# A hybrid encoder layer on one core: one value block in three split, the last key products beside the first score blocks, and pauses ahead of the gate products

## The chip, the cores and the metric

The kernel runs on one core of one Trainium2 chip. The metric is device time in microseconds (us) of one execution, lower is better. The kernel before takes 1352.38 us, the median of three runs (1351.4 to 1353.75).

The core has five engines that work through their own queues in order: TensorE (PE; its weight loads are shown as PEld), VectorE (DVE), ScalarE (ACT), GpSimd (POOL) and SyncE (SP, which only issues transfers here). Sixteen DMA engines move data. TensorE writes to PSUM, the other engines read it from there.

## The reference

One encoder layer is applied to two sequences of 256 tokens of width 1024, with 16 learned tokens put ahead of each. All data are float32.

```python
def layer(h, ...):
    xn = rmsnorm(h, norm_mix_g)
    z = xn @ w_in                                    # convolution gates and inputs, q, k, v
    y_conv = group_rmsnorm(gate_b * depthwise_conv3(gate_c * hc, conv_w), conv_out_g, 8)
    y_attn = group_rmsnorm(gqa_attention(q, k, v), attn_out_g, 8)   # normed, rotated q and k
    h = h + concatenate([y_conv, y_attn]) @ w_out
    return h + peer_ffn(rmsnorm(h, norm_ffn_g), ...)

def peer_ffn(x, wq, subkeys, u_tab, v_tab):          # 8 heads, 128 x 128 experts
    q = (x @ wq).reshape(T, 8, 2, 128)
    s = einsum('thpc,hpnc->thpn', q, subkeys)        # 128 scores for each half of a head
    sv, si = top_k(s, 16)
    cand = sv[..., 0, :, None] + sv[..., 1, None, :]
    cv, cp = top_k(cand, 16)                         # 16 experts of 16384, for each head
    gates = softmax(cv)
    a = gelu(einsum('thkd,td->thk', take(u_tab, eidx), x)) * gates
    return einsum('thk,thkd->td', a, take(v_tab, eidx))
```

The tables u_tab and v_tab hold 16384 rows of 1024 numbers each, 64 MB a table. Each token needs 128 of the experts (8 heads of 16).

## The kernel before

**Two ways to the experts.** The first sequence (two tiles of 128 tokens) gathers: for each tile and each of the 128 picks, one indirect transfer on GpSimd's queue (line 180, tile `grow`) brings for every token the row of u and v of its expert, 128 rows of 8 KB. VectorE then forms the dot product with the token (`grow<-grow,xh`), ScalarE its gelu and the weight (two small instructions on `dots`), and VectorE adds the weighted v row (`xh<-grow,dots,xh`). There are 256 such gathers, and they run in the background of all later stages. Four buffers hold rows in flight (`ring`). A new gather is issued once a buffer is free and TensorE has passed a mark (`sync_dep`, the last matmul that the program had recorded).

The second sequence goes through all experts, with dense matmuls. In the score stage (the loop over `j` that starts at line 975), block j multiplies the 128 experts of row j with the 256 tokens: eight matmuls of 128 x 256, each shown as two records, into one of two PSUM tiles `pSj` that hold four blocks (`SG`). After each fourth block ScalarE takes the gelu of four blocks at once into the big table A (its parts are `Al`, the first 92 blocks, and `Ah`). In the value stage (the loop at line 1023) block j multiplies A(j) with 128 rows of v into four PSUM accumulators `acc`. SyncE brings the weights: `u` in blocks of 512 KB, `v` in pairs of blocks of 1 MB, in three buffers.

**The gates** make the dense way sparse: for each token A is to be multiplied with a matrix that is zero but for its 128 experts. The generator `gates_dense` (line 883) builds it from one-hot matrices. First, `fin1` softmaxes and decodes the picks of both tiles. Then, for each tile of 128 tokens, the index tables are transposed on TensorE (`pi`, `pg`) and copied to `dup`, `ghi` and `glo`. Then come 32 steps of four tokens: VectorE compares (`oi`, `oj`), ScalarE scales (`gh`, `gl`), and a step later TensorE multiplies eight small matrices into `pgm`. After each second step the result is either stored into A (ScalarE, blocks that have no scores yet) or multiplied into A (VectorE, blocks that have).

**What sets the order.** The program issues instructions in the order that it writes them, and a scheduler changes it a little. Background work is paced by credit: `bg(us)`, called after each block with 3.5, gives `us * share["b"]` to the task list (generators, each `yield` names the time that its piece takes) and `us * share["a"]` to the gathers, one per 2.65 of credit. A task's piece therefore lands a number of blocks later that its yields set: with `SBS` = 0.42 a block gives 1.47, so that a yield of 3.0 is worth about two blocks.

**The queries of the second sequence** come ahead of the scores, in `projections` (line 376). For each of 16 half heads, eight matmuls make a query (`pqq`), and two, three half heads later (`lag=3`), the key scores (`pn`, line 385), which ScalarE copies to `Ah`, and after every second of which `step1` puts the top-16 search of a head on VectorE. The three late ones are done after the loop, by `while late`.

**Split value blocks.** Most value blocks use four float32 matmuls of 128 x 512, each shown as two records. Each `SPL`-th block is split instead: ScalarE rounds A(j) and v to the float32r format (`ah`, `vh`, the tile `vhl`), VectorE makes the rests (`al`, `vl`), and TensorE multiplies three terms, twelve float32r matmuls. The splitting of block j is issued one block ahead, ahead of that block's gathers.

Of the kernel before, what the change touches and what calls it, by code (L numbers as in the profile page):

```python
# [8 lines left out]
F32 = mybir.dt.float32  # L9
# [9 lines left out]
P = 128  # L19
# [20 lines left out]
SR = 0.6  # L40
SS = 0.72
SMAX = 0.74
SPL = 4
SBS = 0.42


# [1 line left out]
def encoder_layer(ctx: ExitStack, tc: tile.TileContext, xp, xs_, meta, vec, w_in, w_out, wq,  # L48
# [328 lines left out]
    def projections(xr, sk, scores, qp, step=None, split=False, rescale=None, lag=1):  # L377

        rn = None
        late = []  # L380

        def key_scores(hp, qs):
            pn = pst.tile([P, 2, P], F32, tag="tr", name="pn")
            for t in range(2):
                pe.matmul(pn[:, t, :], qs[:, t * P:(t + 1) * P], sk[:, hp, :], start=True, stop=True)
            if hp < 2 and rn is not None:
                for t in range(2):
                    act.activation(scores[:, hp, t], pn[:, t], AF.Copy, scale=rn[:, t:t + 1])
            else:
                act.activation(scores[:, hp], pn, AF.Copy)  # L390
            if step is not None and hp % 2:
                step(hp // 2)

        for hd in range(PH):
            w = weights(wq, hd, split)
            for pp in range(2):
                pq = psm.tile([P, 256], F32, tag="mm", name="pqq")
                mm(pq, lambda c, k: w(c, k)[:, pp * P:(pp + 1) * P], xr, split=split)
                qs = qp.tile([P, 256], F32, tag="qs", name="qs", bufs=lag + 1)
                act.activation(qs, pq, AF.Copy)  # L400
                late.append((2 * hd + pp, qs))
                if len(late) > lag:
                    key_scores(*late.pop(0))
                if hd == 0 and rescale is not None:
                    rn = rescale(xr, pp)
                bg(3.9)
        while late:
            key_scores(*late.pop(0))


    pf = ExitStack()
# [459 lines left out]
        return rn1  # L871

    share.update(a=SR, b=0.0)
    projections(xr1, sk1, sc1, q1, step1, rescale=rescale, lag=3)
    direct[0] = True
    pfs.close()
    psS = ctx.enter_context(ps("psS", 2))
# [5 lines left out]
    def gates_dense():  # L883

        for t in range(2):
            yield from fin1(t)
        q1x.close()
        topk_left[0] = -1
        yield 10.0
        ogx = ExitStack()  # L890
        og = ogx.enter_context(sb("og", 1, "right"))
        io = og.tile([P, P], F16, name="io")
        act.dma_start(io, iota16)
        ident16 = og.tile([P, P], F16, name="ident16")
        act.activation(ident16, ident, AF.Copy)
        iv = io.rearrange("p (a r) -> p a r", r=2)
        v4 = lambda x: x.rearrange("p t (a r) -> p t a r", r=2)
        steps = []
        pgs = [None]

        def gate_products(a, oi, gh, gl):
            half = a // OC % 2
            if half == 0:
                pgs[0] = psg.tile([P, 2 * OC, P], F32, tag="g", name="pgm")
            pg = pgs[0]
            for r in range(OC):
                q = half * OC + r
                pe.matmul(pg[:, q, :], oi[:, r, :], gh[:, r, :], start=True, stop=False)  # L908
                pe.matmul(pg[:, q, :], oi[:, r, :], gl[:, r, :], start=False, stop=True)  # L909
            if half == 0:  # L910
                return
            a -= OC
            n = r_done[0]
            pj = pg.rearrange("p t j -> p j t")
            parts = [(part, lo, hi, min(max(n, lo), hi)) for part, lo, hi in ((Al, 0, JH), (Ah, JH, P))]
            for part, lo, hi, m in parts:
                if m < hi:
                    act.activation(part[:, m - lo:hi - lo, a:a + 2 * OC], pj[:, m:hi], AF.Copy, scale=1.0 / GSH)
            for part, lo, hi, m in parts:
                if m > lo:  # L920
                    av = part[:, 0:m - lo, a:a + 2 * OC]
                    dve.scalar_tensor_tensor(av, pj[:, lo:m], 1.0 / GSH, av, op0=ALU.mult, op1=ALU.mult)
            tau[0] = a + 2 * OC

        for t in range(2):
            pi = psg.tile([P, 2, P], F16, tag="g", name="pi")
            pe.transpose(pi[:, 0, :], idx_i[:, t], ident16)
            pe.transpose(pi[:, 1, :], idx_j[:, t], ident16)
            pg = psg.tile([P, P], F32, tag="g", name="pg")
            pe.transpose(pg, gate_all[:, 2 + t], ident)  # L930
            glo = og.tile([P, P], F32, tag="glo", name="glo")
            g16 = og.tile([P, OC, P], F16, tag="gl", name="g16", bufs=2)[:, 0, :]
            dup = og.tile([P, 2, P, 2], F16, tag="dup", name="dup")
            ghi = og.tile([P, P], F32, tag="ghi", name="ghi")
            act.activation(g16, pg, AF.Copy, scale=GSH)
            dve.scalar_tensor_tensor(glo, pg, GSH, g16, op0=ALU.mult, op1=ALU.subtract)
            act.activation(ghi, g16, AF.Copy)
            for r in range(2):
                act.activation(dup[:, 0:2, :, r], pi, AF.Copy)
            yield 1.6  # L940
            for o in range(P // OC):
                s0 = o * OC
                oi = og.tile([P, OC, P], F16, tag="oi", name="oi", bufs=2)
                oj = og.tile([P, OC, P], F16, tag="oj", name="oj", bufs=2)
                gh = og.tile([P, OC, P], F16, tag="gh", name="gh", bufs=2)
                gl = og.tile([P, OC, P], F16, tag="gl", name="gl", bufs=2)
                sl4 = lambda k: dup[:, k, s0:s0 + OC, None, :].to_broadcast([P, OC, 64, 2])
                ib = iv[:, None, :, :].to_broadcast([P, OC, 64, 2])
                dve.tensor_tensor(v4(oi), sl4(0), ib, op=ALU.is_equal)
                dve.tensor_tensor(v4(oj), sl4(1), ib, op=ALU.is_equal)  # L950
                for q in range(OC):
                    act.activation(gh[:, q, :], oj[:, q, :], AF.Copy, scale=ghi[:, s0 + q:s0 + q + 1])
                    act.activation(gl[:, q, :], oj[:, q, :], AF.Copy, scale=glo[:, s0 + q:s0 + q + 1])
                steps.append((t * P + s0, oi, gh, gl))
                if len(steps) > 1:
                    gate_products(*steps.pop(0))
                yield 1.3 + (4 * r_done[0] + 60) / 700
        gate_products(*steps.pop(0))
        ogx.close()

    tasks.append(gates_dense())
    share.update(a=SS, b=SBS)
    late = []

    def experts(j, p):
# [12 lines left out]
    for j in range(P):  # L978
# [7 lines left out]
        mm(late[-1][1][:, j % SG], lambda c, k: ub[:, c * P:(c + 1) * P], xr1)  # L986
        if j % SG == 0 and j:
            experts(*late.pop(0))
        bg(3.5)
    experts(*late.pop(0))  # L990
    run_tasks()
# [121 lines left out]
```

## Time and profile before

| | |
|---|---|
| median of three runs | 1352.38 us |
| the profiled execution | 1352.28 us, span 1350.5 us |
| TensorE | busy 1275.4 us (94%), 5998 records |
| VectorE | busy 1043.2 us (77%) |
| ScalarE | busy 536.2 us (40%) |
| GpSimd | busy 387.4 us (29%) |
| granted TensorE clock, mean | 0.984 |
| moved by DMA | 460.19 MB, 341 GB/s over the span |
| chain that ended last | TensorE 51%, DMA 10%, VectorE 8% of the span |

The times count from the start of the span. The first sequence's layer ends with its queries; the second sequence's layer follows, its queries end at 408, the scores run to 924, the values to 1345. Shares over the whole span say little here, since the stages have different limits; stretches and single waits are to be read. In a timeline row the number ahead of the engine is the duration (of several records together where the row ends with a count), and what stands in brackets is the idle time of the engine just before it and what ended it. The record of a matmul is longer than the time between two starts, since matmuls overlap.

### The profile page before, as it was taken

To read this page: it belongs to the slowest core of one execution; us is meant where nothing else is said; L and a number is where in the kernel's file an instruction comes from. 1 tells how busy PE (TensorE), PEld (TensorE's weight loads), DVE (VectorE), ACT (ScalarE), POOL (GpSimd) and SP (SyncE) were. 2 spreads that over 40 slices of the span, in tenths; PEclk is the share of its full clock that TensorE was granted. 3 is DMA by queue.
4 is the path that set the end of the run, shared out by engine and by line. 5 is a ranking of instruction groups with operands and counts; after the bars stand their busy time and mean duration, and the time that the engine had idled before them with its cause. 6 is when DMAs were issued, how large, how long until landed. Compare 5 with 4: busy or idle time off the path is not lost.

```text
span 1350.5 us, 17724 instructions
## 1 busy us (share of the span) xinstructions
PE 1275.4 (94%) x5998; PEld 957.6 (71%) x5998; DVE 1043.2 (77%) x2247; ACT 536.2 (40%) x1576; POOL 387.4 (29%) x480
## 2 busy tenths in 40 slices
PE   5999998888898999779999999998999999999998
PEld 5888996667787887668788888885555555555554
DVE  5656998976699998688887978986767667676665
ACT  4555531752221311176776766641222222222121
POOL 1111124432242334434332322332222223223121
PEclk9999998998998999979999999999999999999999
DMA  5434646576998999999999999999999999999997
GB/s 204 131 103 159 205 123 228 203 267 255 374 326 293 365 418 416 417 383 413 386 405 387 416 408 400 404 413 421 404 403 396 406 401 405 404 395 408 400 402 283
DMA packets 81003, 460.19 MB, mean 341 GB/s; under 512 B 9473, under 2 KB 9985, under 8 KB 39697
## 3 DMA queue, kind: packets, MB, share of 16 engines
q0 software_dynamic: 37296, 270.02, 49.9%
q1 hardware_dynamic: 41888, 183.37, 36.1%
q10 hardware_dynamic: 1728, 5.67, 1.2%
q8 instruction: 47, 0.77, 0.2%
q14 instruction: 44, 0.35, 0.1%
HBM read 454.81 MB, written 4.19 MB: 340 GB/s over the span
## 4 chain that ended last, share of the span: by engine, by line
PE 51%; DMA 10%; DVE 8%; issue 1%; ACT 1%; POOL 0%; DVEq 0%; POOLq 0%
PE acc L1029 30%; PE pSj L138 19%; DMA grow<-in_uv,eidx 10%; DVE Al L65 2%; DVE xh L65 2%; DVE grow L65 2%; PE pgm L908 1%; PE pgm L909 1%; DVE Ah L65 1%; DVE s L65 0%; POOL cd L294 0%; ACT dots L65 0%; DVE c L65 0%; DVE hd L65 0%; ACT gh L65 0%
## 5 line engine op out<-in xcount | busy, mean ns | idle before, releaser
L180 POOL DMA_INDIRECT grow<-in_uv,eidx x256 | 310.6, 1213 | 733.2 <-PE acc L1029 229.7
L138 PE MATMUL pSj<-xr,u 128*128 128x256 f32 x2048 | 468.7, 386 | 4.6 <-ACT Al L65 2.7
L138 PEld LDWEIGHTS pSj<-xr,u 128*128 128x128 f32 x2048 | 387.5, 193 | 62.8 <-DMA u<-in_u_t 6.4
L65 DVE SCALAR_TENSOR_TENSOR grow<-grow,xh 128x1024 f32<-128x1024 f32 x256 | 312.7, 1221 | 143.3 <-DMA grow<-in_uv,eidx 141.9
L65 DVE SCALAR_TENSOR_TENSOR xh<-grow,dots,xh 128x1024 f32<-128x1024 f32 x256 | 328.1, 1282 | 62.9 <-ACT dots L65 61.8
L65 ACT ACTIVATE dots<-dots 128x1 f32<-128x1 f32 x256 | 51.8, 202 | 525.2 <-DVE grow L65 524.3
L1029 PE MATMUL acc<-v,Al 128*128 128x512 f32 x552 | 240.7, 593 | 0.7 <-DMA v<-in_v_n 0.7
L1029 PEld LDWEIGHTS acc<-v,Al 128*128 128x128 f32 x552 | 104.9, 190 | 123.8 <-issue 120.8
L65 ACT ACTIVATE gh<-oj,ghi 128x128 f16<-128x128 f16 x256 | 99.7, 389 | 8.3 <-PE pgm L908 4.7
L65 ACT ACTIVATE gl<-oj,glo 128x128 f16<-128x128 f16 x256 | 99.7, 389 | 0.0
L1029 PE MATMUL acc<-v,Ah 128*128 128x512 f32 x216 | 94.2, 592 | 0.0
L1029 PE MATMUL acc<-vhl,ah 128*128 128x512 f32 x256 | 81.7, 441 | 2.8 <-ACT vhl L65 2.8
L65 ACT ACTIVATE dots<-dots,gate_all 128x1 f32<-128x1 f32 x256 | 74.7, 292 | 6.8
L1029 PEld LDWEIGHTS acc<-v,Ah 128*128 128x128 f32 x216 | 41.1, 190 | 48.0 <-issue 47.3
L1029 PEld LDWEIGHTS acc<-vhl,ah 128*128 128x128 f32 x256 | 48.1, 188 | 26.1 <-issue 14.8
L65 DVE TENSOR_TENSOR wlo<-w,whi 128x1024 fp32r<-128x1024 f32 x42 | 50.9, 1216 | 18.6 <-PE pc L138 11.3
L138 PE MATMUL pqq<-xr,w 128*128 128x256 f32 x256 | 58.1, 380 | 2.9 <-DMA w<-in_wq 1.8
L65 ACT ACTIVATE vhl<-v 128x1024 fp32r<-128x1024 f32 x32 | 33.8, 1056 | 53.9 <-DMA v<-in_v_n 51.4
L138 PEld LDWEIGHTS pqq<-xr,w 128*128 128x128 f32 x256 | 47.6, 190 | 9.3 <-DMA w<-in_wq 2.2
L65 ACT ACTIVATE whi<-w 128x1024 fp32r<-128x1024 f32 x42 | 43.8, 1054 | 17.0 <-PE pqq L138 9.5
L138 PE MATMUL pc<-xT,w 128*128 128x258 f32 (+1 forms) x192 | 47.4, 398 | 2.9 <-DVE rb L65 2.4
L908 PE MATMUL pgm<-gh,oi 128*128 128x128 f16 x256 | 36.3, 221 | 14.1 <-ACT gh L65 11.4
(278 smaller groups left out, 1724.5 us busy)
## 6 DMA issues: line engine op xcount, KB each, us to landing
u<-in_u_t SPq DMA_DIRECT2D x128, 512.0 KB, 8.5
v<-in_v_n SPq DMA_DIRECT2D x64, 1024.0 KB, 9.1
w<-in_w_in SPq DMA_DIRECT2D x36, 512.0 KB, 4.6
w<-in_wq SPq DMA_DIRECT2D x32, 512.0 KB, 4.7
w<-in_w_out SPq DMA_DIRECT2D x16, 512.0 KB, 4.0
grow<-in_uv,eidx POOLq DMA_INDIRECT x256, 9.7
hdram<-h ACTq DMA_DIRECT2D x3, 512.0 KB, 4.1
h<-in_xp SPq DMA_DIRECT2D x2, 512.0 KB
```

The costliest lines, as they stand in the source:

```text
L65: i = f(*a, **k)
L138: i = pe.matmul(out, st_(c, a), mv(c, b), start=(n == 0), stop=(n == NC * len(terms) - 1))
L180: i = pool.indirect_dma_start(out=r, out_offset=None, in_=uv, in_offset=bass.IndirectOffsetOnAxis(ap=eidx[:, t, k:k + 1], axis=0))
L908: pe.matmul(pg[:, q, :], oi[:, r, :], gh[:, r, :], start=True, stop=False)
L909: pe.matmul(pg[:, q, :], oi[:, r, :], gl[:, r, :], start=False, stop=True)
L1029: i = pe.matmul(acc[t][q], a[:, t * P:(t + 1) * P], v[:, q * 512:(q + 1) * 512], start=j == 0 and n == 0, stop=j == P - 1 and n == len(ter ...
```

## The change

Three edits. (1) `SPL` becomes 3: value blocks 2, 5, 8, ..., 125 are split, 42 in place of 32. (2) `projections` with a lag over 1 returns its late key scores as a function; the score loop calls it after blocks 0, 1 and 2, into the PSUM pool of the gates. The gates task and its shares are set after block 3. (3) The yield ahead of the gates' tables falls from 10 to 6, and two yields are added for each tile of tokens, 3.0 ahead of its first step and 2.0 behind its first step.

```diff
-SPL = 4
+SPL = 3
...
-        def key_scores(hp, qs):
-            pn = pst.tile([P, 2, P], F32, tag="tr", name="pn")
+        def key_scores(hp, qs, pl=None, tag="tr"):
+            pn = (pl or pst).tile([P, 2, P], F32, tag=tag, name="pn")
...
-        while late:
-            key_scores(*late.pop(0))
+        if lag > 1:
+            return lambda pl, tag: late and key_scores(*late.pop(0), pl, tag)
+        key_scores(*late.pop(0))
...
-    projections(xr1, sk1, sc1, q1, step1, rescale=rescale, lag=3)
+    rest = projections(xr1, sk1, sc1, q1, step1, rescale=rescale, lag=3)
...
         topk_left[0] = -1
-        yield 10.0
+        yield 6.0
...
             yield 1.6
+            yield 3.0
             for o in range(P // OC):
...
                     gate_products(*steps.pop(0))
+                if o == 0:
+                    yield 2.0
                 yield 1.3 + (4 * r_done[0] + 60) / 700
...
-    tasks.append(gates_dense())
-    share.update(a=SS, b=SBS)
     late = []
...
             experts(*late.pop(0))
+        if j < 3:
+            rest(psg, "g")
+        if j == 3:
+            tasks.append(gates_dense())
+            share.update(a=SS, b=SBS)
         bg(3.5)
```

What this does to the order is read from the two programs. First TensorE, from the first score block to the second set of gate products of the first tile (`pSj` x8 is one score block, `pi` and `pg` are the transposes, `pgm` the gate products). Before:

```order
L138 MATMUL pSj<-xr,u 128x256 x312
L927 LDWEIGHTS idx_i
L927 MATMUL pi<-ident_5105,idx_i 128x128
L928 LDWEIGHTS idx_j
L928 MATMUL pi<-ident_5105,idx_j 128x128
L930 MATMUL pg<-ident,gate_all 128x128
L138 MATMUL pSj<-xr,u 128x256 x16
L908 LDWEIGHTS oi
L908 MATMUL pgm<-gh,oi 128x128
```

After, with the last key scores (`pn`) among the first blocks:

```order
L138 MATMUL pSj<-xr,u 128x256 x16
L385 MATMUL pn<-Ah,qs 128x128
L138 MATMUL pSj<-xr,u 128x256 x8
L385 MATMUL pn<-Ah,qs 128x128 x2
L138 MATMUL pSj<-xr,u 128x256 x296
L928 LDWEIGHTS idx_i
L928 MATMUL pi<-ident_5103,idx_i 128x128
L929 LDWEIGHTS idx_j
L929 MATMUL pi<-ident_5103,idx_j 128x128
L931 MATMUL pg<-ident,gate_all 128x128
L138 MATMUL pSj<-xr,u 128x256 x40
L909 LDWEIGHTS oi
```

One more score block stands ahead of the transposes (40, not 39) and five stand between them and the first gate products, where two stood. The key scores, of which two instructions make a half head, come behind blocks 1 and 2 in part.

On ScalarE the same place is the one where the transposes' results are copied (`dup`, `ghi`); `Al<-pSj` is the gelu of blocks 36 to 39, each pair of `dots` belongs to one gather, `gh` and `gl` are the scalings of the first step. Before:

```order
L65 ACTIVATE dots<-dots 128x1
L65 ACTIVATE dots<-dots,gate_all 128x1
L65 ACTIVATE dup<-pi 128x256
L65 ACTIVATE g_5113<-pg 128x128
L65 ACTIVATE dup<-pi 128x256
L65 ACTIVATE ghi<-g_5113 128x128
L65 ACTIVATE dots<-dots 128x1
L65 ACTIVATE dots<-dots,gate_all 128x1
L65 ACTIVATE Al<-pSj 128x1024
L65 ACTIVATE dots<-dots 128x1
L65 ACTIVATE dots<-dots,gate_all 128x1
L65 ACTIVATE gh<-oj,ghi 128x128
```

After:

```order
L65 ACTIVATE dots<-dots 128x1
L65 ACTIVATE dots<-dots,gate_all 128x1
L65 ACTIVATE Al<-pSj 128x1024
L65 ACTIVATE g_5111<-pg 128x128
L65 ACTIVATE dup<-pi 128x256
L65 ACTIVATE ghi<-g_5111 128x128
L65 ACTIVATE dup<-pi 128x256
L65 ACTIVATE dots<-dots 128x1
L65 ACTIVATE dots<-dots,gate_all 128x1
L65 ACTIVATE dots<-dots 128x1
L65 ACTIVATE dots<-dots,gate_all 128x1
L65 ACTIVATE gh<-oj,ghi 128x128
```

The copies of the transposes stood ahead of that gelu and now stand behind it; counted from the gelu of blocks 32 to 35, four gathers' pairs stood ahead of it and now five do; and two pairs stand between the copies and the first scaling, as before.

The third place is VectorE at the change from scores to values. `Al<-pgm` and `Ah<-pgm` multiply gate products into A, `Ah<-pSj` multiplies the gelu of new blocks with the gates that are there, `al` and `vhl` are the rests of the first split value block. Before, from the last gate products on:

```order
L65 SCALAR_TENSOR_TENSOR Al<-pgm,Al 128x92x8
L65 SCALAR_TENSOR_TENSOR Ah<-pgm,Ah 128x28x8
L65 SCALAR_TENSOR_TENSOR xh<-grow,dots,xh 128x1024
L65 SCALAR_TENSOR_TENSOR grow,dots<-grow,xh 128x1024
L65 TENSOR_TENSOR al<-Al,ah 128x256
L65 SCALAR_TENSOR_TENSOR xh<-grow,dots,xh 128x1024
L65 SCALAR_TENSOR_TENSOR grow,dots<-grow,xh 128x1024
```

After:

```order
L65 SCALAR_TENSOR_TENSOR grow,dots<-grow,xh 128x1024
L65 SCALAR_TENSOR_TENSOR xh<-grow,dots,xh 128x1024
L65 SCALAR_TENSOR_TENSOR grow,dots<-grow,xh 128x1024
L65 SCALAR_TENSOR_TENSOR Al<-pgm,Al 128x92x8
L65 SCALAR_TENSOR_TENSOR xh<-grow,dots,xh 128x1024
L65 SCALAR_TENSOR_TENSOR grow,dots<-grow,xh 128x1024
L65 TENSOR_TENSOR Ah<-pSj,Ah 128x4x248
L65 SCALAR_TENSOR_TENSOR Ah<-pgm,Ah 128x36x8
L65 TENSOR_TENSOR al<-Al,ah 128x256
L65 TENSOR_TENSOR vhl<-v,vhl 128x1024
L65 SCALAR_TENSOR_TENSOR xh<-grow,dots,xh 128x1024
```

Before, nine gathers' pairs and the gelu products of eight blocks came between the last gate products and the first `vhl`; now one pair does, and the last gate products stand at the very end of the score stage.

## Rows read from the trace of the kernel before

**Rows 1.** Stretches: length, PE, PEld, DVE, ACT, POOL busy (records), clock, DMA share, GB/s.

```profile
480.00:560.00 80.00, 78.87 (x348) 63.98 (x347) 66.55 (x96) 14.81 (x49) 35.07 (x22) 1.00 1.02 416
560.00:585.00 25.00, 10.63 (x37) 7.54 (x36) 20.06 (x28) 9.57 (x33) 10.58 (x8) 0.73 1.01 410
920.00:960.00 40.00, 36.57 (x105) 19.38 (x104) 27.87 (x34) 9.44 (x26) 9.14 (x9) 1.00 1.01 419
960.00:1320.00 360.00, 360.00 (x997) 188.69 (x996) 244.65 (x305) 77.80 (x219) 94.47 (x83) 1.00 1.00 402
480.00:1320.00 840.00, 818.34 (x3361) 569.11 (x3360) 646.18 (x904) 333.56 (x1095) 256.00 (x209) 0.99 1.00 404
```

**Rows 2.** Timeline of TensorE, last key scores: start, us, operation, count, idle time ahead.

```profile
412.18 2.93 PE L385 MATMUL pn<-Ah,qs 128*128 128x128 f32 x12 [3.46 <-ACT Ah L65]
415.58 4.76 PE L138 MATMUL pSj<-xr,u 128*128 128x256 f32 x16 [0.47 <-ACT Ah L65]
```

**Rows 3.** Timeline of TensorE around the first gate products.

```profile
564.46 5.41 PE L138 MATMUL pSj<-xr,u 128*128 128x256 f32 x16 [2.73 <-ACT Al L65]
...
581.31 0.27 PE L908 MATMUL pgm<-gh,oi 128*128 128x128 f16 x1 [11.44 <-ACT gh L65]
...
583.42 9.59 PE L138 MATMUL pSj<-xr,u 128*128 128x256 f32 x32
...
593.29 3.67 PE L138 MATMUL pSj<-xr,u 128*128 128x256 f32 x16
```

**Rows 4.** Timeline of ScalarE in the same place.

```profile
559.54 0.20 ACT L65 ACTIVATE dots<-dots 128x1 f32<-128x1 f32 x1 [3.21 <-DVE grow L65]
...
563.29 0.20 ACT L65 ACTIVATE dots<-dots 128x1 f32<-128x1 f32 x1 [3.23 <-DVE grow L65]
563.40 1.01 ACT L65 ACTIVATE Al<-pSj 128x1024 f32<-128x1024 f32 x1
...
580.87 0.39 ACT L65 ACTIVATE gh<-oj,ghi 128x128 f16<-128x128 f16 x1
```

**Rows 5.** Timeline of TensorE at the second hole.

```profile
640.32 3.67 PE L138 MATMUL pSj<-xr,u 128*128 128x256 f32 x16
646.33 0.24 PE L908 MATMUL pgm<-gh,oi 128*128 128x128 f16 x1 [2.34 <-DVE oi L65]
...
647.11 5.02 PE L138 MATMUL pSj<-xr,u 128*128 128x256 f32 x16
```

**Rows 6.** Timeline of TensorE, change from scores to values.

```profile
899.12 24.39 PE L138 MATMUL pSj<-xr,u 128*128 128x256 f32 x112
924.16 10.57 PE L1029 MATMUL acc<-v,Al 128*128 128x512 f32 x24 [0.65 <-DMA v<-in_v_n]
937.51 1.21 PE L1029 MATMUL acc<-vhl,ah 128*128 128x512 f32 x4 [2.77 <-ACT vhl L65]
```

**Rows 7.** Timeline of VectorE, the last gate products multiplied into A.

```profile
900.30 0.91 DVE L65 SCALAR_TENSOR_TENSOR Al<-pgm,Al 128x736 f32<-128x736 f32 x1
```

**Rows 8.** Timeline of TensorE, one period of four value blocks.

```profile
953.46 10.46 PE L1029 MATMUL acc<-v,Al 128*128 128x512 f32 x24
963.36 1.48 PE L1029 MATMUL acc<-vhl,ah 128*128 128x512 f32 x4
964.68 1.08 PE L1029 MATMUL acc<-vhl,al 128*128 128x512 f32 x4
...
966.51 1.02 PE L1029 MATMUL acc<-v,Al 128*128 128x512 f32 x2
```

**Rows 9.** Timeline of ScalarE and VectorE, the splitting for that period.

```profile
956.20 1.06 ACT L65 ACTIVATE vhl<-v 128x1024 fp32r<-128x1024 f32 x1 [0.74 <-DMA v<-in_v_n]
...
959.16 1.22 DVE L65 TENSOR_TENSOR vhl<-v,vhl 128x1024 fp32r<-128x1024 f32 x1
960.29 0.42 DVE L65 TENSOR_TENSOR al<-Al,ah 128x256 fp32r<-128x256 f32 x1
```

**Rows 10.** Transfers issued: engine, count, size, median us from issue to landing.

```profile
v<-in_v_n SPq DMA_DIRECT2D x64, 1024.0 KB, 9.1
```

## What I predicted

> **What bounds the kernel now.** I read the table of stretches first [rows 1]. From 480 to 1320 us TensorE is busy for 818.34 of 840 us and the DMA engines are full too, at 404 GB/s. Two limits lie on top of each other, and the question for any edit is which of them has room. From 960 to 1320 TensorE is busy all the time: the value stage is bound by its matmuls. From 560 to 585 it is busy for 10.63 of 25 us, and there is the only large hole.
>
> Next I read TensorE in order of time around that hole [rows 3]. Score block 40 starts 2.73 us late, for ScalarE; the first gate product waits 11.44 us more; and the two score blocks from 583.42 take 9.59 us, where one block is recorded at 3.67 [rows 5]. The granted clock of 560 to 585 is 0.73, so part of this stretch runs at the lower of the two levels, behind idle time. The place costs 2.73 + 11.44 + (9.59 - 7.34) = 16.4 us. A smaller hole follows [rows 5]: 2.34 us of waiting and a block of 5.02 us in place of 3.67, 3.7 us in all.
>
> Then ScalarE in the same place [rows 4]. It works in order. Between its large evictions (the gelu of four score blocks, 1.01 us) stands a small pair of instructions for each gather, which waits for VectorE, which waits for the gather's transfer. These pairs come 3.75 us apart (559.54, 563.29), which with the score weights beside them is about the 416 GB/s of 480 to 560 [rows 1], the highest rate that holds for long. So ScalarE runs late, TensorE has only two buffers of four score blocks, and it stands until ScalarE comes. The hole is TensorE's, and DMA makes it.
>
> Last I read the change of stages [rows 6, 7] and one period of the value stage [rows 8, 9].
>
> **The change part by part.** The sum is made against the profiled execution, 1352.28 us (span 1350.5 and 1.78 around it). The median of the runs shown is 1352.38, so one number serves for both.
>
> *Key products.* Before, the last of them hold TensorE from 412.18 to 415.58 [rows 2], 3.4 us, since each pair waits for ScalarE to empty one of two PSUM tiles. Now five instructions of key scores stand ahead of the first block, not eight, and three come between the first blocks (order on TensorE); the first block should start near 413.5. I cost the 1 to 2 us won at nothing: at block 40 TensorE waits for ScalarE anyway [rows 3], whose date comes from the gathers, and in ScalarE's order 68 gathers stand ahead of the gelu of blocks 32 to 35 in both kernels. Bounds: 2 us won (the wait at block 40 gone), 1 lost (top-k work on VectorE that gets its scores three blocks later).
>
> *Start of the gates.* The transposes come after 40 blocks, not 39, and the first gate products after 45, not 41. The gelu of blocks 32 to 35 ends at 564.4 as before, so block 40 starts there in both. Blocks 40 to 43 then fill TensorE until about 579, in the place of the long wait. Block 44 needs the gelu of blocks 36 to 39, which now has five gather pairs ahead of it, not four: 563.29 + 5 x 3.75 = 582.0, so block 44 starts near 583.3 after a wait of 4 us, and ends at 587. The first gate products need the scalings gh, which stand two gathers later, 582.0 + 7.5 = 589.5, and from the first scaling to the end of the set it takes 583.42 - 580.87 = 2.5 us: 592.0, with 45 blocks done. Before, block 45 began at 593.29 + 2 x 3.92 = 601.1 (3.92 from the 12 blocks between 593.29 and 640.32 [rows 3, 5]), with three more sets of gate products done, 3.92 - 3.48 = 0.44 each (3.48 from seven blocks without them in 24.39 us [rows 6]). So 601.1 - 592.0 - 1.3 = 7.8 us are won of 16.4.
>
> What is late next is the same chain. The second hole stands behind 92 gathers before; at the same block 89 stand ahead now (order on ScalarE), since a longer task lets gathers slip. Three gathers of 3.75 us are 11.2 us of relief, so what is won can be kept, but the 3.7 us are hardly closed as well. To the end of the scores 3 to 4 gathers fewer stand ahead of each gelu. I take 8 us. Bounds: 0 (ScalarE decides as before) and 16.4 + 3.7 = 20.1 (both holes gone).
>
> *Queues that are passed.* Gathers on GpSimd are held by marks of TensorE, and score weights on SyncE by buffers that TensorE frees; both follow it and come earlier by what it wins. Behind ScalarE's wait for the transposes' result stand gather pairs; they wait there before as well.
>
> *End of the scores.* The gates' last step, which stood seven blocks ahead of the values, now stands directly ahead of them (order on VectorE). Before, the change of stages cost 0.65 us for DMA and 2.77 us for ScalarE, 3.4 us [rows 6]. Now the first value block needs the last gate product and VectorE's multiply of 0.91 us [rows 7], behind up to two gathers in VectorE's order; the first split block is one block nearer to the start, but while TensorE waits for the multiply its copy can be made. I put both at 3.4 us, the difference at 0, since the 3.4 is the nearest row. Bounds: 3.4 won, and 8 lost (a wait as the 11.44 us at the first gate products).
>
> *Value blocks.* 42 blocks are split, not 32. In the split block the last eight matmuls take 966.51 - 964.68 = 1.83 us, 0.23 each, so twelve take 2.75. The period of four blocks is 966.51 - 953.46 = 13.05 us, so an unsplit block takes (13.05 - 2.75) / 3 = 3.43 us [rows 8]. Ten blocks at 0.68 are 6.8 us. Read by starts alone (963.36 - 953.46 = 9.90 for three, 3.15 for one) it would be 10 x 0.15 = 1.5 us. I take the first reading, since a start at a change of kind seems recorded early.
>
> The Trainium skill (FP8 and Floating Point Precision, section TensorE Precision Notes) says that true FP32 takes four passes through the array. By it three terms would take 3/4 of 3.43 us, and ten blocks would save 8.6 us; the 2.75 us measured are more than that 2.57, and the measurement is taken.
>
> What the splits cost: each adds 1.06 us on ScalarE and 1.22 + 0.42 on VectorE [rows 9], 11 and 16 us in a stage where these are busy 77.80 and 244.65 of 360 us: covered. But blocks 2, 8, 14, ... are the first of a pair that one transfer brings; before, the split one was always the second. In [rows 9] the pair landed at 956.20, VectorE had the last part at 960.71, 4.5 us later, and TensorE came to it at 963.36. The pair's first block was due 3.43 us sooner, at 959.93, and its second term 0.9 later, at 960.85. So at 21 places the margin falls to some 0.1 us, and I count 0.1 us lost at each. DMA: a block needs 0.524 MB of values and 97/126 of a gather of 1.049 MB in 9.61/3 = 3.20 us, 416 GB/s, where 94/126 in 3.26 us made 401 (402 measured). 416 and 419 are the highest rates of [rows 1], so it just fits. I take 4 us won; bounds 6.8 won, 5 lost (0.55 us at each of 21 places).
>
> **Sum:** 0 + 8 + 0 + 4 = 12 us; 1352.3 - 12 = 1340 us.
>
> **Rivals.** *DMA takes it all back.* For it: full engines at 404 GB/s. Against: 416 holds for 80 us. If 404 is the most that this mixture gives, each wait returns elsewhere, and the time is 1352. If 416 is, the room is 840 x (1 - 404/416) = 24 us, above the sum. Chance 0.11.
>
> The Trainium skill (HBM Reference, section Specifications (TRN2)) gives about 425 GB/s to a core that streams alone. By it the room would be 42 us; no row here shows more than 419.
>
> *The pauses do too little.* ScalarE is no earlier against TensorE, because its gathers decide; only the values gain: 1352.3 - 4 = 1348. Against: four blocks of work do lie in the hole now. Chance 0.12.
>
> *All holes close.* 20.1 + 6.8 + 1, cut to the room of 24 us: 1328. Against: 73 gathers cannot be served by 579. Chance 0.14.
>
> *Slower: split blocks that come first in their pair starve.* It decides as soon as a pair lands about 1 us later against its use than in [rows 9]: 10 us after its issue where the median is 9.1 [rows 10]. At 1.2 us at each of 21 places 25 us are lost against 8 + 6.8 won: 1363. Against: a TensorE that waits frees DMA, so that the next pair lands sooner. Chance 0.07.
>
> **How the numbers follow.** The forecast has 0.56. The range, 1328 to 1352, reaches from all holes closed to nothing won; perhaps 0.07 lie below and 0.11 above. The likeliest case alone spans 1334 to 1346. A difference under 0.2%, 2.7 us, cannot be told from none. Faster: 0.56 + 0.14 + 0.10 of the second rival = 0.80. Same: 0.10 of the first and 0.02 of the second, 0.12. Slower: 0.07 and 0.01 of the first, 0.08.
>
> **What would show it.** In the changed profile the wait of 11.44 us at the first gate products should be gone, with one of 3 to 5 us at block 44 and one of 3 to 5 us at the first gate product in its place. The first score block starts near 413.5, and block 40 still near 564. The value stage lasts some 416 us where it lasted 420, at DMA rates of 410 to 419. Wrong would be: a wait of over 8 us at the start of the values; many short waits of TensorE for vhl or al; or block 40 itself earlier or later by more than 3 us.

## The result and the profile after

The changed kernel takes 1347.88 us, the median of 20 runs, where the kernel before took 1355.24 us beside it (20 runs). The ratio is 0.995, with a 95% interval of 0.9934 to 0.9966: by the ratio 6.8 us won, 4.6 to 8.9 by the interval (the two medians lie 7.4 apart). I had forecast 12. The direction was right and the measured time lies inside the range, but the size was wrong. The profiled execution took 1349.14 us, its span is 1347.4, 3.1 us below the one before.

The table of stretches of the changed kernel answers to [rows 1]; one stretch is added (900 to 920).

```profile
480.00:560.00 80.00, 78.83 (x349) 64.92 (x348) 66.72 (x96) 15.19 (x48) 32.89 (x21) 1.00 1.02 416
560.00:585.00 25.00, 19.82 (x83) 16.56 (x82) 17.79 (x22) 6.31 (x20) 12.09 (x8) 0.86 1.02 417
900.00:920.00 20.00, 19.74 (x121) 17.25 (x119) 18.09 (x27) 13.16 (x46) 5.86 (x6) 1.00 0.91 340
920.00:960.00 40.00, 32.76 (x87) 17.67 (x88) 27.76 (x36) 8.76 (x27) 9.63 (x8) 0.87 0.92 368
960.00:1320.00 360.00, 359.57 (x1041) 196.40 (x1041) 263.07 (x331) 89.71 (x244) 96.09 (x86) 1.00 1.01 413
480.00:1320.00 840.00, 818.94 (x3409) 579.27 (x3408) 659.41 (x926) 344.89 (x1112) 257.57 (x209) 0.99 1.00 405
```

Between 560 and 585 TensorE is busy for 19.82 us, before for 10.63: most of the hole is filled. Between 900 and 920 DMA moves 340 GB/s, where the kernel before moved 417. Between 920 and 960 TensorE is busy for 32.76, before for 36.57, and DMA has fallen from 419 to 368 GB/s: a new hole, and not one that full DMA engines make.

TensorE around the first gate products, where [rows 3] showed the wait of 11.44 us (bracket: idle time ahead and what ended it):

```profile
566.30 16.37 PE L138 MATMUL pSj<-xr,u 128*128 128x256 f32 x64 [4.34 <-ACT Al L65]
583.52 3.72 PE L138 MATMUL pSj<-xr,u 128*128 128x256 f32 x16 [0.84 <-ACT Al L65]
590.43 0.22 PE L909 MATMUL pgm<-gh,oi 128*128 128x128 f16 x1 [3.19 <-ACT gh L65]
592.53 4.83 PE L138 MATMUL pSj<-xr,u 128*128 128x256 f32 x16
...
642.18 7.13 PE L138 MATMUL pSj<-xr,u 128*128 128x256 f32 x32
```

Blocks 40 to 43 now run through what was the wait, slowly: 16.37 us for four, with a granted clock of 0.86 from 560 to 585. Waits of 4.34 us (block 40, before 2.73), 0.84 (block 44, which starts at 583.52) and 3.19 (the first gate product, at 590.43) are left. The last row stands where the second hole was [rows 5]; there is none, two blocks take 7.13 us.

ScalarE in the same place, against [rows 4]: the gelu of blocks 36 to 39 and the first scaling.

```profile
582.46 1.00 ACT L65 ACTIVATE Al<-pSj 128x1024 f32<-128x1024 f32 x1
...
589.99 0.39 ACT L65 ACTIVATE gh<-oj,ghi 128x128 f16<-128x128 f16 x1
```

The change from scores to values, against [rows 6]: TensorE, from the last gate product to the first split block.

```profile
919.52 0.22 PE L910 MATMUL pgm<-gl,oi 128*128 128x128 f16 x1
927.24 9.86 PE L1036 MATMUL acc<-v,Al 128*128 128x512 f32 x16 [7.50 <-DMA v<-in_v_n]
936.54 1.50 PE L1036 MATMUL acc<-vhl,ah 128*128 128x512 f32 x4
...
949.34 7.03 PE L1036 MATMUL acc<-v,Al 128*128 128x512 f32 x16
955.80 1.48 PE L1036 MATMUL acc<-vhl,ah 128*128 128x512 f32 x4
957.12 1.08 PE L1036 MATMUL acc<-vhl,al 128*128 128x512 f32 x4
958.04 1.08 PE L1036 MATMUL acc<-vhl,ah 128*128 128x512 f32 x4
958.96 7.03 PE L1036 MATMUL acc<-v,Al 128*128 128x512 f32 x16
```

Where 0.65 us of waiting for `v` stood, 7.50 us stand now. The first two value blocks also take 9.30 us (927.24 to 936.54), and two later ones 6.46 (949.34 to 955.80), 2.8 more. From 949.34 on, one period of three blocks takes 958.96 - 949.34 = 9.62 us.

Why `v` came late is read from SyncE. Its first issue of `v` in the timeline of the kernel before:

```profile
910.16 13.71 SPq L1009 DMA_DIRECT2D v<-in_v_n  x3
```

In the changed kernel, its longest wait between 900 and 930 us (total, times, longest), and the issue in the timeline:

```profile
SPq L1016 <- PE pgm L910: 15.4, 1, 15.4
```

```profile
919.81 1.46 SPq L1016 DMA_DIRECT2D v<-in_v_n  x3
```

Before, the first pair was issued at 910.16, right behind the last score weights and 13.4 us ahead of the scores' end at 923.51. Now it waits 15.4 us for the last gate product and leaves at 919.81, when the scores are over. The addresses in the program say why. The gates' pool lies at 148416 to 159168 bytes of each partition, and the first of the three `v` buffers at 150976 to 159168, in that same memory. Before, the gates were done seven blocks earlier, so the lock (as I call the wait of a new tile for the last use of its memory) was open by the time SyncE came to it.

VectorE in the same place, against [rows 7]:

```profile
921.53 0.92 DVE L65 SCALAR_TENSOR_TENSOR Al<-pgm,Al 128x736 f32<-128x736 f32 x1
...
924.70 1.18 DVE L65 TENSOR_TENSOR Ah<-pSj,Ah 128x992 f32<-128x992 f32 x1
925.80 0.45 DVE L65 SCALAR_TENSOR_TENSOR Ah<-pgm,Ah 128x288 f32<-128x288 f32 x1
```

The accumulators `acc` lie in the PSUM that the `pgm` tiles leave, so the first value product also has to wait until VectorE has read the last of these. The last multiply out of it ends at 926.25, only 1.0 us ahead of TensorE's start. A second lock stands right behind the first.

### The profile page after: what moved, and what is told of

It reads as the page before. It is cut to its first block, busy times and chain, and to the rows that moved or that the text cites. A ratio compares the mean times of both kernels' runs of the same rounds, so it can differ in the third digit from the quotient of the medians.

```text
span 1347.4 us, 17821 instructions
## 1 busy us (share of the span) xinstructions
PE 1278.2 (95%) x6038; PEld 971.0 (72%) x6038; DVE 1056.6 (78%) x2269; ACT 546.3 (41%) x1593; POOL 388.7 (29%) x480
## 4 chain that ended last, share of the span: by engine, by line
PE 42%; DMA 13%; DVE 11%; issue 2%; ACT 2%; POOL 0%; SPq 0%; DVEq 0%; POOLq 0%; ACTq 0%
PE acc L1036 21%; PE pSj L138 20%; DMA grow<-in_uv,eidx 12%; DVE xh L65 4%; DVE grow L65 2%; DVE Al L65 2%; DMA v<-in_v_n 2%; PE pgm L910 1%; PE pgm L909 1%; DVE vhl L65 1%; DVE Ah L65 1%; ACT dots L65 1%; ACT vhl L65 1%; DVE s L65 0%; POOL cd L294 0%
## 5 line engine op out<-in xcount | busy, mean ns | idle before, releaser
L1036 PE MATMUL acc<-v,Al 128*128 128x512 f32 x496 | 220.7, 599 | 7.5 <-DMA v<-in_v_n 7.5
L1036 PEld LDWEIGHTS acc<-v,Al 128*128 128x128 f32 x496 | 95.3, 192 | 115.5 <-issue 113.0
L1036 PE MATMUL acc<-vhl,ah 128*128 128x512 f32 x336 | 107.1, 441 | 0.1
L65 DVE TENSOR_TENSOR vhl<-v,vhl 128x1024 fp32r<-128x1024 f32 x42 | 51.5, 1225 | 56.4 <-ACT vhl L65 56.2
L1036 PEld LDWEIGHTS acc<-vhl,ah 128*128 128x128 f32 x336 | 63.1, 188 | 30.9 <-issue 18.6
L1036 PE MATMUL acc<-v,Ah 128*128 128x512 f32 x192 | 84.4, 592 | 0.0
L1036 PEld LDWEIGHTS acc<-v,Ah 128*128 128x128 f32 x192 | 36.5, 190 | 41.1 <-issue 40.1
L138 PE MATMUL pc<-xT,w 128*128 128x258 f32 (+1 forms) x192 | 50.5, 417 | 2.9 <-DVE rb L65 2.4
L65 ACT ACTIVATE vhl<-v 128x1024 fp32r<-128x1024 f32 x42 | 44.0, 1047 | 19.2 <-DMA v<-in_v_n 17.4
```

The lines of the kernel that those rows point to most:

```text
L65: i = f(*a, **k)
L138: i = pe.matmul(out, st_(c, a), mv(c, b), start=(n == 0), stop=(n == NC * len(terms) - 1))
L1036: i = pe.matmul(acc[t][q], a[:, t * P:(t + 1) * P], v[:, q * 512:(q + 1) * 512], start=j == 0 and n == 0, stop=j == P - 1 and n == len(ter ...
```

## The experiments

My theory after the two traces: the gates' late end costs some 7 us at the start of the values and eats about half of what the other two edits win. The rival: full DMA engines take back whatever is won, wherever. All ten kernels ran in five rounds beside the kernel before.

**Splits alone, in the kernel before.**

```diff
-SPL = 4
+SPL = 3
```

> The kernel before with 42 split value blocks and nothing else. Theory A (the first pair of value rows lies in SBUF that the gates' tiles hold, so it can be issued only after the last gate product): here the gates end seven blocks early as before, so the first pair is issued near 910 us, TensorE waits under 1 us for it, and the first split block (block 2) waits 2 to 6 us for vhl; from block 4 to the end the value stage takes about 400 us instead of 404; in all 1 to 4 us faster than before, ratio 0.997 to 0.999. Rival B (the DMA engines are full, so that further splits win nothing): the stage from block 4 on takes 404 us, ratio 1.000.

Measured: 1345.08 us, ratio 0.9917 [0.9895, 0.9939], 11 us won. That is more than either theory said, and more than the whole change; B falls, and A's number with it. In its trace TensorE enters the values without a wait. The wait of 2.77 us for the first split block [rows 6] is gone, but one of 2.28 us stands at the third, block 8, the first of its pair:

```profile
923.14 7.13 PE L1029 MATMUL acc<-v,Al 128*128 128x512 f32 x16
930.22 1.19 PE L1029 MATMUL acc<-vhl,ah 128*128 128x512 f32 x4
...
953.33 1.81 PE L1029 MATMUL acc<-vhl,al 128*128 128x512 f32 x4 [2.28 <-DVE al L65]
```

**The changed kernel without the added splits.**

```diff
-SPL = 3
+SPL = 4
```

> The changed kernel with 32 split blocks, so key products and pauses alone. Theory A: about 4 us are won by the end of the scores (the wait of 11.4 us at the first gate products is replaced by waits of 1 to 4 us at three places), and 6 to 8 us are lost waiting for the first value pair, which is issued only behind the last gate product; ratio to before 0.999 to 1.003. Rival C (the wait for the value pair is a matter of that one execution): no such wait, ratio 0.996 to 0.998.

Measured: 1354.54 us, 1.0005 [0.9985, 1.0024]. Key products and pauses, with the late end that the pauses bring, come out even. TensorE waits 7.83 us for `v` here too; rival C falls.

**A late end alone, in the kernel before**: the pause stands ahead of the second tile only, so the first hole stays and the gates end directly ahead of the values.

```diff
-            yield 1.6
+            yield 1.6 + 10.0 * t
```

> The kernel before with a pause of 10 units ahead of the second tile's gate steps only, so that the first gate products stand where they stood (the hole of 11.4 us stays) and the last gate products stand directly ahead of the values. Theory A: the first value pair is issued only behind the last gate product, TensorE waits 6 to 8 us for it where it waited 0.65, and the time is 3 to 7 us longer than before, ratio 1.002 to 1.005. Rival D (the pair comes late because the queues are full of gathers, not because of its buffer): it is issued near 910 us as before, the wait stays under 2 us, ratio 1.000.

Measured: 1364.03 us, 1.0075 [1.0047, 1.0102], 10 us lost: A's direction, and more than A's numbers, whose upper end the interval just touches. TensorE at its start of the values:

```profile
925.98 0.22 PE L909 MATMUL pgm<-gl,oi 128*128 128x128 f16 x1
934.36 12.53 PE L1029 MATMUL acc<-v,Al 128*128 128x512 f32 x24 [8.16 <-DMA v<-in_v_n]
```

SyncE waits 15.4 us for the last gate product here too, so D falls. The late end makes the wait without any other part of the change.

**The changed kernel with pauses for the first tile only**; the last gate products stand three blocks ahead of the values.

```diff
-            yield 3.0
+            if t == 0:
+                yield 3.0
...
-                if o == 0:
+                if t == 0 and o == 0:
                     yield 2.0
```

> The changed kernel with the two pauses at the first tile of the gates only, so that the last gate products stand three blocks ahead of the values. Theory A: the wait for the first value pair falls from 7.5 us to 0 to 3 us, and the kernel is 4 to 7 us faster than the changed one, ratio to before 0.990 to 0.993. Rival D (full queues): the wait stays at 6 to 8 us, ratio as the changed kernel's, 0.995.

Measured: 1341.62 us, 0.9901 [0.9879, 0.9924], as A said. SyncE issues the first pair 10 us ahead of need, and TensorE has no wait there; D falls again:

```profile
904.40 30.37 SPq L1017 DMA_DIRECT2D v<-in_v_n  x6
```

```profile
904.17 10.58 PE L138 MATMUL pSj<-xr,u 128*128 128x256 f32 x48
914.58 7.03 PE L1037 MATMUL acc<-v,Al 128*128 128x512 f32 x16
```

**The late end kept, the first pair in other memory.**

```diff
-    vp = ctx.enter_context(sb("vp", 3, "right"))
+    vq = ctx.enter_context(sb("vq", 1, "right"))
+    vp = ctx.enter_context(sb("vp", 2, "right"))
...
-            vpair[0] = vp.tile([P, 2, D], F32, tag="v", name="v")
+            vpair[0] = (vp if j % 6 else vq).tile([P, 2, D], F32, tag="v", name="v")
```

> The changed kernel, but the first, fourth, ... value pair gets its own buffer at the top of the region that the score weights leave, so that the first pair no longer lies in the memory of the gate products; nothing else differs. Theory A (the first pair is issued late because its buffer is freed by the last gate product): it can now be issued at the end of score block 126, one block of 3.5 us ahead of the end, so the wait at the first value block falls from 7.5 to about 4 us, and the time is 1344 to 1345, 0.991 to 0.993 of the kernel before where the changed kernel has 0.995. Rival B (the pair lands when the DMA engines have room, whenever it is issued): the wait stays 6 to 8 us and the ratio 0.995.

Measured: 1346.89 us, 0.9927 [0.9903, 0.9952], not to be told from the changed kernel: the ratio lies in A's range, and the interval holds B's 0.995, so the trace has to decide. Theory A got the issue right and the wait wrong. SyncE, TensorE and VectorE:

```profile
916.75 5.19 SPq L1017 DMA_DIRECT2D v<-in_v_n  x3
```

```profile
928.16 8.66 PE L1037 MATMUL acc<-v,Al 128*128 128x512 f32 x16 [7.09 <-DVE Ah L65]
```

```profile
920.99 1.28 DVE L65 SCALAR_TENSOR_TENSOR xh<-grow,dots,xh 128x1024 f32<-128x1024 f32 x1 [0.60 <-ACT dots L65]
922.20 1.22 DVE L65 SCALAR_TENSOR_TENSOR grow<-grow,xh 128x1024 f32<-128x1024 f32 x1
...
923.34 0.92 DVE L65 SCALAR_TENSOR_TENSOR Al<-pgm,Al 128x736 f32<-128x736 f32 x1
924.17 1.27 DVE L65 SCALAR_TENSOR_TENSOR xh<-grow,dots,xh 128x1024 f32<-128x1024 f32 x1
925.37 1.22 DVE L65 SCALAR_TENSOR_TENSOR grow<-grow,xh 128x1024 f32<-128x1024 f32 x1
...
926.51 1.18 DVE L65 TENSOR_TENSOR Ah<-pSj,Ah 128x992 f32<-128x992 f32 x1
927.62 0.45 DVE L65 SCALAR_TENSOR_TENSOR Ah<-pgm,Ah 128x288 f32<-128x288 f32 x1
```

The pair leaves 4.3 us ahead of the scores' end (921.07), and what ends the wait is no longer `v` but the second lock: the last multiply out of `pgm` ends at 928.07, behind two gathers' pairs in VectorE's order. So the cause is the late end with both of its locks, not the buffer alone. Rival B's number for the wait came, but not by its mechanism: VectorE ends this wait, not a transfer. No kernel moved the second lock alone, so what each lock costs by itself is not shown.

**An end eight blocks early**: the kernel with pauses for the first tile only, and

```diff
-                yield 1.3 + (4 * r_done[0] + 60) / 700
+                yield 1.2 + (4 * r_done[0] + 60) / 700
```

> As the kernel with pauses for the first tile only (0.990), and each gate step's price 1.2 in place of 1.3, so that the last gate products stand eight score blocks ahead of the values, as far as in the kernel before. Theory A: the first value pair already came in time there, so nothing more is won at the start of the values; the steps press a little more on the first gate products: 0.989 to 0.992. Rival D (a gate product costs TensorE waits wherever the steps are dense, and the earlier end brings them back): 0.993 to 0.996.

Measured: 1344.12 us, 0.9909 [0.9886, 0.9933]. Eight blocks of distance cannot be told from three.

**The changed kernel with its key products back ahead of the first block.**

```diff
-        if lag > 1:
-            return lambda pl, tag: late and key_scores(*late.pop(0), pl, tag)
-        key_scores(*late.pop(0))
+        while late:
+            key_scores(*late.pop(0))
...
-        if j < 3:
-            rest(psg, "g")
```

> The changed kernel with all key products ahead of the first score block again (pauses, splits and the late end of the gates kept). Theory A (the key products are worth the 1 us by which the first score block starts earlier, and nothing behind it): 0.995 to 0.997. Rival E (the gain at the first gate products hangs on them, since gathers and gelus shift against each other): 0.998 to 1.001.

Measured: 1346.49 us, 0.9931 [0.9908, 0.9954], even a little below the changed kernel's 0.995, with overlapping intervals. The interval reaches A's lower end; E falls.

**The changed kernel with the old price and no pauses.**

```diff
-        yield 6.0
+        yield 10.0
...
-            yield 3.0
...
-                if o == 0:
-                    yield 2.0
```

> The changed kernel with the price of 10 ahead of the gates and no pauses (splits and moved key products kept); the last gate products stand four blocks ahead of the values and the first 41 blocks deep. Theory A (without the pauses the hole of 11 us at the first gate products is back, 5 us in all, but the late end that costs 7 is gone too): 0.990 to 0.993, about as the kernel before with the splits alone (0.992). Rival F (the pauses are what wins, and their late end costs little): 0.997 to 1.000.

Measured: 1344.89 us, 0.9926 [0.9901, 0.9951], as A said. The first gate products stand behind 44 blocks here, not behind 41 as expected, but two blocks behind the transposes, as in the kernel before. TensorE waits 12.74 us for them again:

```profile
592.55 0.26 PE L909 MATMUL pgm<-gh,oi 128*128 128x128 f16 x1 [12.74 <-ACT gh L65]
```

The values start without a wait. F falls.

**Pauses for the first tile, splits, key products as before.** The edit is that of the key products above, made in the kernel with pauses for the first tile only.

> The kernel with pauses for the first tile only (0.990), with all key products ahead of the first score block again. Theory A (with the pauses the 2.7 us by which the first score block starts earlier are lost again before the gates begin, since ScalarE's gathers set the date): 0.989 to 0.991. Rival E (the 2.7 us are kept to the end): 0.992 to 0.993.

Measured: 1339.29 us, 0.9879 [0.9853, 0.9906]. The interval holds most of A's range, and E falls; moving the key products wins nothing here either.

**Every second block split**, in the kernel with pauses for the first tile only.

```diff
-SPL = 3
+SPL = 2
```

> The kernel with pauses for the first tile only (0.990), with every second value block split, 64 in place of 42. Theory A (TensorE alone bounds the value stage, as it is busy all the time there): 22 more splits of 0.68 us win 15 us, 0.979. Theory G (the transfers are the next bound: with every third block split 960 to 1320 us already runs at 416 GB/s, and no stretch of a trace showed more than 419 to 422): 3 us at most, 0.987 to 0.990.

Measured: 1337.91 us, 0.9878 [0.9848, 0.9909]: G holds, A (0.979) falls. The value stage, with every third and with every second block split:

```profile
960.00:1320.00 360.00, 360.00 (x1049) 198.00 (x1048) 267.14 (x337) 90.84 (x248) 95.83 (x85) 1.00 1.01 416
```

```profile
960.00:1320.00 360.00, 356.65 (x1126) 209.12 (x1125) 292.11 (x374) 113.54 (x286) 107.74 (x86) 1.00 1.01 417
```

The rate stands still at 417 GB/s, and TensorE begins to idle. The waits recorded are those for the splitting: in this stretch TensorE's weight loads wait 14.0 us (26 times) for ScalarE's `ah` and 10.0 us (22 times) for VectorE's `al`; with every third block split they wait for neither. That the transfers stand behind these engines is argued from the rate; no run separates the two. This kernel and the one ahead of it are the fastest of the study, 15 to 16 us below the kernel before.

## Why the prediction was wrong

Single executions begin the scores up to 9 us apart, so I read each trace from two points of its own: from the start of the last query on TensorE to the end of scores and gates, and from there to the end of the last value product (us; late end: last gate products directly ahead of the values).

| kernel | last query starts | scores end | between | values end | from scores' end |
|---|---|---|---|---|---|
| before | 404.65 | 923.51 | 518.9 | 1345.22 | 421.7 |
| splits alone | 403.20 | 923.14 | 519.9 | 1339.06 | 415.9 |
| late end alone | 405.43 | 926.20 | 520.8 | 1354.31 | 428.1 |
| changed (late end) | 406.37 | 919.74 | 513.4 | 1343.45 | 423.7 |
| changed, no added splits (late end) | 405.08 | 916.43 | 511.4 | 1344.75 | 428.3 |
| changed, first pair elsewhere (late end) | 407.83 | 921.07 | 513.2 | 1341.05 | 420.0 |
| changed, keys back (late end) | 407.51 | 919.90 | 512.4 | 1339.75 | 419.9 |
| pauses for the first tile | 404.25 | 914.58 | 510.3 | 1328.41 | 413.8 |
| end eight blocks early | 412.20 | 923.31 | 511.1 | 1338.15 | 414.8 |
| pauses back | 403.45 | 919.65 | 516.2 | 1333.68 | 414.0 |
| pauses and splits, keys back | 409.14 | 923.91 | 514.8 | 1338.19 | 414.3 |

**Start of the gates: right in size.** Forecast 8 us. Five traces with pauses and moved keys give 510.3 to 513.4, 511.9 in the mean, against 519.9 in the three with neither: 8.0 us (5.5 between the two traces of before and after alone, 6.3 for the two with pauses and the keys in place). The dates came as written: block 44 at 583.52 (583.3 forecast), its gelu at 582.46 (582.0), the first scaling at 589.99 (589.5), the end of the first set of gate products at 592.53 (592.0). Block 40 was 1.8 us later than before, as its execution's last query was (406.37 against 404.65). Of the two waits of 3 to 5 us that I expected, the one at the first gate product came (3.19); at block 44 it was 0.84, since blocks 40 to 43 ran slow. But that 8 us were kept to the end is in part luck. Counted from the last query, the changed kernel leads by 10.4 us at block 45 (592.53 against 601.20), which is 9.1 when the three sets of gate products still to be done are taken off, as in the forecast. At block 50 it leads by 4.25 us (618.45 against 620.98), and by 2.5 without the four sets: a wait of 2.05 us at the third set of gate products (603.37), and slow blocks and gate products around it, have taken the rest. At block 58 the lead is 8.5 us (649.59 against 656.37), since the kernel before has its second hole in between. I had left that hole open; it is gone, and its closing makes good what was lost.

**Key products: forecast 0, and 0 by the times.** The first block starts 8.25 us after the last query, before 10.93. These 2.7 us are lost within three blocks, since the first two run slow behind a wait of 3.52 us (10.21 us, where two take 7.13), with a granted clock of 0.69 from 414 to 425:

```profile
414.62 10.21 PE L138 MATMUL pSj<-xr,u 128*128 128x256 f32 x32 [3.52 <-ACT Ah L65]
```

Block 3 starts 22.4 us after the last query in both kernels, and block 40 at 159.9, before 159.8 (159.0 to 161.0 in all twelve traces). So block 40 keeps its date, as I wrote, but the lead was gone long before it came to that wait. With the keys moved or not, the ratios are 0.9926 and 0.9917 without pauses, 0.9950 and 0.9931 with the late end, 0.9901 and 0.9879 with pauses for the first tile. No pair shows a gain; all three lean the other way, with overlapping intervals.

**End of the scores: here the prediction failed.** I "put both at 3.4 us, the difference at 0". The step took 7.50 us of waiting and 2.8 in slow blocks, 10.3 in all. An early end is not free either: before, it cost the 3.4 us, and with 42 splits TensorE waits 1.2 to 2.3 us for the first split blocks. In the table the late end costs 428.2 - 421.7 = 6.5 us with 32 splits, and with 42 the mean of three, 421.2 (419.9 to 423.7), less that of five, 414.6 (413.8 to 415.9): 6.6. The times say 10 us alone (6 to 14 by the interval) and 6.6 inside the change (0.9950 against 0.9901). I had named the gathers ahead of the multiply, and a bound of 8 lost that holds it. But I took the nearest row, 3.4 us, although its distance of seven blocks was exactly what the change removed. And under the queues that are passed I had said of SyncE's transfers that they come earlier, without asking whose memory the first `v` lands in; in the list of waits of before, SyncE does not wait for the gates there, because that lock was long open. My mark for "wrong" was a wait of over 8 us; 7.50 came, and it was as telling.

**Value blocks: too low.** I took 4 of the 6.8 us that the splits save on TensorE and gave 2.8 to small waits, 2.1 of them by the working (21 places at 0.1), 0.7 without a reason. Of ScalarE's work for a split I had left out `ah`, 0.40 us each; there was room for it. From the table: 421.7 - 414.6 = 7.1 with an early end, 428.2 - 421.2 = 7.0 with a late one. The periods agree: 13.05 us for four blocks before [rows 8], 9.62 for three now, so 128 x (3.263 - 3.207) = 7.2. Blocks that come first in their pair did not starve: after the first split the changed kernel's TensorE shows one wait in the whole stage, of 0.19 us. Two such places, blocks 8 and 14, on ScalarE and VectorE, against [rows 9]:

```profile
950.12 1.04 ACT L65 ACTIVATE vhl<-v 128x1024 fp32r<-128x1024 f32 x1
...
970.29 1.06 ACT L65 ACTIVATE vhl<-v 128x1024 fp32r<-128x1024 f32 x1 [1.66 <-DMA v<-in_v_n]
```

```profile
951.19 1.23 DVE L65 TENSOR_TENSOR vhl<-v,vhl 128x1024 fp32r<-128x1024 f32 x1 [1.54 <-ACT vhl L65]
952.33 0.42 DVE L65 TENSOR_TENSOR al<-Al,ah 128x256 fp32r<-128x256 f32 x1
...
976.24 0.42 DVE L65 TENSOR_TENSOR al<-Al,ah 128x256 fp32r<-128x256 f32 x1
```

At block 8 the pair was there in time and VectorE was done at 952.75, TensorE came at 955.80. At block 14 the pair landed at 970.29, `al` was done at 976.66, and TensorE, which came at 975.04, waited the 0.19 us for its second term. So the margin does shrink to nothing at times, as I wrote. All small losses, most without a recorded wait, do come to about the 2.1 us that I had counted in this execution: five periods of three blocks behind the first nine are 0.2 to 0.7 us longer than 9.62, 2.3 us in all. In the other seven traces with 42 splits they are 0.0 to 0.2 us; what makes them in this one is open.

**The sum:** 0 + 8.0 - 6.6 + 7.1 = 8.5 us by the traces, 6.8 (4.6 to 8.9) by the times. The terms are means over several kernels; the two traces of before and after alone give 518.9 - 513.4 + 421.7 - 423.7 = 3.5 us. Without the late end the change wins 13.4 us (10.3 to 16.4), so the forecast of 12 fits a kernel that ends its gates three blocks sooner, not this one.

**The rivals.** That DMA takes it all back is refuted for this change: splits alone win 11 us. It fits one step further: the next 22 splits, worth 15 us on TensorE, win 3 (0.9901 to 0.9878, with overlapping intervals). That the pauses do too little gave the right time, 1348, by luck, for another reason: the pauses do their work at the first gates, and lose it at the last. What stays open is the exact size of their gain: 8 us in the traces, but 1 to 5 in the times of kernels with splits and an early end (0.9909, 0.9901 and 0.9879, against 0.9917 for the splits alone), whose intervals are 3 us wide to either side. With 32 splits and the late end in both, key products and pauses win 9.5 us in the times (1.0005 against 1.0075, intervals apart) and 9.4 in the traces (511.4 against 520.8); why less of it shows with 42 splits is open.

## What to carry to other kernels

When a change moves the last use of a piece of memory, list what lies there next: a transfer that was free to start early takes on the new date, and it is in no list of waits of before, since its lock was already open. Price such a place by the distance that is removed, not by what the place costs now. And test parts of a change in pairs, with and without each other: here two parts that each win and one side effect that loses made a small sum, and moving the gates' end by three blocks gave back 6.6 us.

## What the runs showed of the hardware

After a wait of 7 to 8 us TensorE also ran slow for a while, in all five traces that have such a wait at the start of the values. In the changed kernel the granted clock from 920 to 940 is 0.74, so part of it is at the lower of the two levels (1.2 and 2.4 GHz):

```profile
920.00:940.00 20.00, 12.76 (x29) 6.68 (x30) 12.58 (x17) 3.21 (x11) 3.31 (x3) 0.74 0.87 344
```

Behind the wait of 7.50 us this cost 2.8 us, behind 7.83 us (no added splits) three blocks took 11.81 us where three took 9.90 later, 1.9 more; behind the other three it cost 1.6 to 2.1. I had counted such slow blocks in the holes of before, but not in the bound of 8 us for a wait at the start of the values. And with every second value block split 417 GB/s held over 360 us, where I had 416 over 80 us to go by.
